# Both closing meetings of the engines placed ahead of GpSimd's wait for the last store

The kernel runs on one core of a Trainium2 chip (trn2). The metric is the time of one execution in device microseconds; each time of a kernel is a median of four to six runs (of the kernel before, up to eleven), and each stamp of a trace comes from one profiled run. All runs are fast (recorded clock 1.00).

## The reference

```python
def reference(x, y):            # both 1024 x 4096, float32
    z = x + y
    return (0.5 * z * (1 + np.tanh(np.sqrt(2 / np.pi) * (z + 0.044715 * z ** 3)))).astype(np.float32)
```

An addition and a GELU: 33.55 MB are read, 16.78 MB written.

## The kernel before

The arithmetic is split into 32 chunks of 128x1024: GpSimd adds (the first chunk is VectorE's), ScalarE squares and takes the sigmoid, VectorE does the two products. All loads and all five stores are issued by SyncE. None of this is touched. What is touched is the end of the program, which the framework writes and the kernel edits after compiling:

```python
    stores = [8192, 8192, 8192, 4096, 4096]      # elements per partition; the last is 2 MB in all
    ...
def wait_late(nc):
    body, end = nc.main_func.blocks[1:3]
    last = [i for i in body.instructions if isinstance(i, mybir.InstDMACopy)][-1]
    (sem,) = [u.id for u in last.sync_info.on_update]       # the last store's semaphore
    all_done = end.instructions[0]                           # SyncE's wait for everything
    clear = next(i for i in end.instructions if isinstance(i, mybir.InstDrain) and i.is_reset_sema)
    ...
    its = [w for w in waits if w.id == sem]
    rest = [w for w in waits if w.id != sem]
    ...
    at = end.instructions.index(clear)
    end.instructions[0] = drain(all_done, rest, is_reset_sema=False)
    end.instructions[at] = drain(clear, its, is_reset_sema=True, ...)
```

So the end block reads as follows. "Meeting" means: each of four engines adds 1 to a semaphore (96) and waits for another (97); GpSimd waits for the four, then releases them. In the trace of before the second meeting's four adds stand at 115.649 to 115.732 and the record of GpSimd's release at 120.430.

| SyncE | ScalarE, VectorE, TensorE | GpSimd |
|---|---|---|
| waits for all stores but the last | | |
| first meeting | first meeting | first meeting |
| | | drain that waits for the last store (semaphore 108) |
| | | range clear of semaphores 99 to 109 |
| second meeting | second meeting | second meeting: a drain, a wait for four, a release |

Behind that block the trace shows semaphore updates that match no record of the program: in the trace of before nine of semaphore 2 (120.769 to 121.294), one of each of the semaphores 7 to 255, but for a single missing record (121.193 to 121.860), and nine more of semaphore 2 (122.085 to 122.442). In all that follows, these are called the runtime's meeting (or first round), the sweep and the runtime's second round. The trace has no record of who makes these updates or what for.

## Time and profile before

| | before |
|---|---|
| three runs | 122.04, 122.37, 122.44 us |
| span, first to last instruction | 120.5 us |
| share of the DMA engines that the one queue fills | 98.1% |
| last increment of the last store | 120.013 |
| GpSimd's last record ends | 120.447 |
| last record of the span ends (TensorE) | 120.534 |
| runtime's first nine updates | 120.769 to 121.294 |
| runtime's second nine updates | 122.085 to 122.442 |

The stamps are starts or ends of records in the trace, in us from the start of the span. The last store's semaphore (108) gets 16 increments in the trace; at the last of them the store counts as landed here. It came 0.380 us after the last 16 KB packet's end (119.633 to 120.013). The last four rows are the tail in which no data moves. The measured time runs to about the last update of semaphore 2: in the profiled run the last update stood at 122.442 and the time was 122.32. So the tail counts in the measured time, beyond what the span shows.

### The profile page before, as it was taken

To read this page: it belongs to the slowest core of one execution; us is meant where nothing else is said; L and a number is where in the kernel's file an instruction comes from. 1 tells how busy PE (TensorE), PEld (TensorE's weight loads), DVE (VectorE), ACT (ScalarE), POOL (GpSimd) and SP (SyncE) were. 2 spreads that over 40 slices of the span, in tenths; PEclk is the share of its full clock that TensorE was granted. 3 is DMA by queue.
4 is the path that set the end of the run, shared out by engine and by line. 5 is a ranking of instruction groups with operands and counts; after the bars stand their busy time and mean duration, and the time that the engine had idled before them with its cause. 6 is when DMAs were issued, how large, how long until landed. Compare 5 with 4: busy or idle time off the path is not lost.

```text
span 120.5 us, 247 instructions
## 1 busy us (share of the span) xinstructions
DVE 75.5 (63%) x66; ACT 63.8 (53%) x66; POOL 73.0 (61%) x35
## 2 busy tenths in 40 slices
DVE  0044700059999009999996999995999999500000
ACT  4016200078875048788758888883878888100000
POOL 0056000699990299999979999949999990000000
DMA  6999999989898989898989899999999999998994
GB/s 201 430 457 449 440 416 446 468 381 489 348 522 348 522 348 522 348 511 359 500 370 489 381 478 391 359 402 459 394 468 402 468 402 468 391 478 364 430 435 174
DMA packets 2162, 50.35 MB, mean 418 GB/s; under 512 B 240, under 2 KB 240, under 8 KB 240
## 3 DMA queue, kind: packets, MB, share of 16 engines
q1 hardware_dynamic: 2160, 50.33, 98.1%
q14 instruction: 2, 0.02, 0.0%
HBM read 33.55 MB, written 16.78 MB: 418 GB/s over the span
## 4 chain that ended last, share of the span: by engine, by line
DMA 49%; POOL 17%; DVE 16%; SPq 1%; ACT 1%; issue 0%; POOLq 0%
DMA y<-in_y_dram 49%; POOL z L131 17%; DVE z L151 8%; DVE w L142 8%; ACT w L136 1%; SPq L114 1%; SPq L121 0%; POOLq L131 0%
## 5 line engine op out<-in xcount | busy, mean ns | idle before, releaser
L131 POOL TENSOR_TENSOR z<-z,y 128x1024 f32<-128x1024 f32 x31 | 72.8, 2387 | 26.3 <-DMA y<-in_y_dram 26.3
L142 DVE SCALAR_TENSOR_TENSOR w<-w,z 128x1024 f32<-128x1024 f32 x32 | 39.4, 1232 | 21.3 <-ACT w L136 21.3
L136 ACT ACTIVATE w<-z 128x1024 f32<-128x1024 f32 x32 | 32.9, 1028 | 37.5 <-POOL z L131 31.6
L151 DVE TENSOR_TENSOR z<-w,z 128x1024 f32<-128x1024 f32 x32 | 38.8, 1215 | 0.0
L147 ACT ACTIVATE w<-w 128x1024 f32<-128x1024 f32 x32 | 31.4, 981 | 0.4 <-DVE w L142 0.4
L131 DVE TENSOR_TENSOR z<-z,y 128x1024 f32<-128x1024 f32 x1 | 1.2, 1226 | 6.0 <-DMA y<-in_y_dram 6.0
L190 ACT ACT_TABLE_LOAD x1 | 1.3, 1283 | 1.3 <-PEq L222 1.3
L189 DVE MEMSET one<- 128x1 f32 x1 | 0.1, 59 | 1.3 <-PEq L222 1.3
L222 POOL MEMSET const-float32-0.0<- 128x1 f32 x1 | 0.1, 98 | 0.2 <-issue 0.2
L190 ACT ACTIVATE one<-one 128x1 f32<-128x1 f32 x1 | 0.2, 203 | 0.0
L222 POOL MEMSET const-bfloat16-1.0<- 128x1 bf16 x1 | 0.1, 101 | 0.0
L222 POOL MEMSET const-uint8-127<- 128x1 uint8 x1 | 0.1, 101 | 0.0
L222 POOL MEMSET const-float32-1.0<- 128x1 f32 x1 | 0.1, 98 | 0.0
## 6 DMA issues: line engine op xcount, KB each, us to landing
z<-in_x_dram SPq DMA_DIRECT2D x3, 4096.0 KB, 34.1
y<-in_y_dram SPq DMA_DIRECT2D x3, 4096.0 KB, 24.8
out_dram<-z SPq DMA_DIRECT2D x3, 4096.0 KB, 30.6
out_dram<-z SPq DMA_DIRECT2D x2, 2048.0 KB, 17.5
z<-in_x_dram SPq DMA_DIRECT2D x1, 3072.0 KB, 13.4
y<-in_y_dram SPq DMA_DIRECT2D x1, 3072.0 KB, 20.3
z<-in_x_dram SPq DMA_DIRECT2D x1, 1024.0 KB, 4.9
y<-in_y_dram SPq DMA_DIRECT2D x1, 1024.0 KB, 6.9
```

What stands on the lines that cost most here:

```text
L114: nc.sync.dma_start(out=zt[:, a:b], in_=xv[:, a:b])
L131: eng.tensor_add(out=zt[:, a:b], in0=zt[:, a:b], in1=yt[s][:, o : o + b - a])
L136: nc.scalar.activation(out=wt[c], in_=zt[:, a:b], func=act.Square, scale=root)
L142: nc.vector.scalar_tensor_tensor(out=wt[c], in0=wt[c], scalar=c1, in1=zt[:, a:b], op0=alu.add, op1=alu.mult)
L147: nc.scalar.activation(out=wt[c], in_=wt[c], func=act.Sigmoid)
L151: nc.vector.tensor_mul(out=zt[:, a:b], in0=wt[c], in1=zt[:, a:b])
L189: nc.vector.memset(one, 0.0)
L190: nc.scalar.activation(out=one, in_=one, func=act.Sigmoid)
L222: nc = _bacc.Bacc("TRN2", target_bir_lowering=False, num_devices=1)
```

## The change

Its intent: with the last store's wait and the clear behind both meetings, the second meeting can take place while the last store still runs, and GpSimd has only these two instructions left once it has landed. (The diffs here are cut; `...` stands for what is left out of a line.)

```diff
     at = end.instructions.index(clear)
+    clears = [drain(clear, its, is_reset_sema=True, ...), end.instructions[at + 1]]
+    assert isinstance(clears[1], mybir.InstISA) and clears[1].engine == POOL
+    del end.instructions[at : at + 2]
     end.instructions[0] = drain(all_done, rest, is_reset_sema=False)
-    end.instructions[at] = drain(clear, its, is_reset_sema=True, ...)
+    end.instructions.extend(clears)
```

More of the change, by code (lines that the diff above doesn't have):

```diff
@@ L47, in wait_late @@
     at = end.instructions.index(clear)
+    clears = [
+        drain(
+            clear, its, is_reset_sema=True,
+            reset_range_start=clear.reset_range_start, reset_range_stop=clear.reset_range_stop,
+        ),
+        end.instructions[at + 1],
+    ]
+    assert isinstance(clears[1], mybir.InstISA) and clears[1].engine == POOL
+    del end.instructions[at : at + 2]
     end.instructions[0] = drain(all_done, rest, is_reset_sema=False)
-    end.instructions[at] = drain(
-        clear, its, is_reset_sema=True,
-        reset_range_start=clear.reset_range_start, reset_range_stop=clear.reset_range_stop,
-    )
+    end.instructions.extend(clears)
 @with_exitstack
```

## The prediction

> **What bounds the kernel now.** I read the page from the top: span, engine shares, queues; then the busy time by stretch, the waits of the SyncE queue, and last every instruction of the closing line (L205), because that is all the change touches.
>
> ```profile
> span 120.5 us, 247 instructions
> DVE 75.5 (63%) x66; ACT 63.8 (53%) x66; POOL 73.0 (61%) x35
> ...
> q1 hardware_dynamic: 2160, 50.33, 98.1%
> ```
>
> No engine is busy for two thirds of the span, but the one DMA queue fills 98.1% of what 16 DMA engines have. 33.55 MB are read and 16.78 MB written, at 418 GB/s: the kernel is bound by its traffic, and the engines keep up. The busy time by stretch says it by stage (columns: stretch, length, DVE, ACT and POOL busy, clock, DMA share, GB/s):
>
> ```profile
> 0.00:104.50 104.50, 75.52 (x66) 63.76 (x66) 73.02 (x35) 1.00 1.00 425
> 104.50:120.04 15.54, 0.00 (x0) 0.00 (x0) 0.00 (x0) 1.00 0.89 384
> 120.04:120.60 0.56, 0.00 (x0) 0.00 (x0) 0.00 (x0) 1.00 0.00 0
> ```
>
> All arithmetic is over at 104.5. For 15.54 us the stores alone run. After that there are 0.56 us in which nothing moves and nothing computes: only sequencers talk. That last stretch is all that this change can reach inside the span. The page's chain that ended last stops at the last VectorE multiply (104.16), since it does not follow the sequencers, so it is of no use here. The waits of the SyncE queue are:
>
> ```profile
> SPq L125 <- DVE z L151: 42.1, 4, 19.7
> SPq L121 <- POOL z L131: 32.6, 2, 18.6
> SPq L121 <- DMA y<-in_y_dram: 22.7, 3, 14.6
> SPq L205 <- DMA out_dram<-z: 10.6, 2, 5.8
> SPq L205 <- PEq L205: 5.0, 2, 4.9
> ```
>
> The fourth row is SyncE waiting for the third-to-last and second-to-last stores at the end (5.8 and 4.8 us). The fifth is the wait in question: about 4.9 us in the second meeting of the engines, before its release (the engine named is only the last to arrive). The true holder is GpSimd, which waits for the last store before it goes to that meeting. The records of L205 from 120.03 on (durations in ns, first and last start in us):
>
> ```profile
> L205 POOLq DRAIN  x2: 34/58/83, 120.0 to 120.3; - x2
> L205 POOLq EVENT_SEMAPHORE  x2: 17/17/17, 120.4 to 120.4; - x2
> L205 POOLq EVENT_SEMAPHORE_RANGE_CLEAR  x1: 95/95/95, 120.1 to 120.1; - x1
> L205 SPq EVENT_SEMAPHORE  x1: 17/17/17, 120.5 to 120.5; - x1
> L205 ACTq EVENT_SEMAPHORE  x1: 17/17/17, 120.5 to 120.5; - x1
> L205 DVEq EVENT_SEMAPHORE  x1: 21/21/21, 120.5 to 120.5; - x1
> L205 PEldq EVENT_SEMAPHORE  x1: 51/51/51, 120.5 to 120.5; - x1
> ```
>
> With the stamps of the single records in the trace, the tail reads so. The last of the 16 increments of the last store comes at 120.013. GpSimd's waiting drain begins at 120.037 (83 ns), the clear at 120.149 (95 ns) and ends at **120.244**. Then GpSimd's own drain at 120.273 (34 ns), its wait for the four arrivals at 120.351 (17 ns; they came at 115.7), its release at 120.430 (17 ns, ends at 120.447). Then the four others leave: SyncE 120.471, ScalarE 120.475, VectorE and TensorE 120.483, the last ending at **120.534**.
>
> [...] after the kernel semaphore 2 gets nine updates from 120.769 to 121.294 (525 ns), then a sweep of semaphores, then nine from 122.085 to 122.442 (357 ns). The profiled run's time was 122.32 us, 1.8 more than its span, so I take this tail to be in the measured time. [...] GpSimd's three records between clear and release sum to 68 ns (34+17+17), but take 203 ns of time (120.244 to 120.447). So I count by starts and ends, not by durations. [...] the last 16 KB packet ended at 119.633 and the last increment came 380 ns later. The change leaves that alone.
>
> **The change part by part.** Nothing is removed or added: the built programs have the same instructions, apart from their order. On GpSimd two of them (the drain that waits for the last store, the range clear) go from between the meetings to the end. On the other four engines no order changes.
>
> 1. Up to the first meeting: nothing moves. All loads, arithmetic, stores and SyncE's waits stay; 0 us.
> 2. The second meeting now follows the first at once. In the trace before, the four arrive for it at 115.640 to 115.711, last increment 115.732. GpSimd's release follows some 0.1 us later, as in the first meeting (wait at 115.429, release ended 115.524). So everyone leaves by about 115.95 (estimate). This runs beside the last store, which lands 4 us later: free.
> 3. After the last store GpSimd has only the drain and the clear: by the stamps above it ends at 120.244. Taken off its path: 120.447 - 120.244 = **0.203 us**. Taken off the span, where TensorE's record ended last: 120.534 - 120.244 = **0.290 us**, so a span of 120.24.
> 4. The runtime's meeting follows. In its first round of semaphore 2 the gap between the second and third update is 205 ns, against 38 ns in the round with nobody late: one engine came 167 ns late. I can't see which. If it was GpSimd, its way from 120.447 to 121.008 takes 0.561 us; it stays on the path whole, and the gain is GpSimd's own 0.203. If it was another, that one now arrives 4.5 us early, and only GpSimd counts: with a way as short as 0.235 (TensorE's end at 120.534 to the first update at 120.769, an assumption) it arrives at 120.479, the rest of a round from its third update takes 0.285 (122.157 to 122.442), and the round ends at 120.764 in place of 121.294, a gain of 0.53.
>
> So 0.20 to 0.53 us, and I choose the span's own 0.29 as the middle, nearer the low end because GpSimd has the slowest drains (34 to 83 ns against 7 to 19 ns of the others) and is the likeliest late one. 122.37 - 0.29 = 122.08, which I put at **122.1 us**, 0.2% faster.
>
> **The rivals.** First: nothing at all is gained, because the runtime meets all the engines again anyway, and the second meeting's release is merely replaced by that. For it: the four others now wait in the runtime's meeting instead of the kernel's. Against it: GpSimd must pass both in series today, 0.203 us of which go. It would make 122.37. Second: the gain is much larger, since four engines could do their closing work (0.24 us for TensorE, the sweep of semaphores of 0.67 us from 121.193 to 121.860) under the store. For: they are idle for 4.5 us. Against: the sweep begins only once the runtime's meeting has GpSimd in it. If it did overlap, some 0.7 us more would go: 121.4. Third: it slows, because four engines go on to write or fetch through the DMA engines while the last store runs; a 32-byte fetch takes 7 ns in the trace and an 8 KB instruction page 309 to 559 ns on one of 16 engines. Two of these in the last 4 us would hardly show; at worst, if a page fell on the engine that lands last, +0.3 us: 122.4. Fourth: the traffic itself varies. The three times span 122.04 to 122.44, 0.40 us, larger than the effect; this can hide it but is no cause.
>
> **Range and chances.** Mechanism 0.20 to 0.53, the median's scatter about 0.2 each way: 121.75 to 122.45 should hold 8 times in 10. Two per cent are 2.4 us. All time in which no data moves after the last landing is 0.52 us in the span and 1.9 in the runtime's tail (120.534 to 122.442), so a gain over 2% would need all of it; a loss over 2% would need a store disturbed by 2.4 us, for which nothing speaks. Faster 0.01, same 0.98, slower 0.01.
>
> **What would show it.** Step 2: both meetings' records of L205 on SyncE, ScalarE, VectorE and TensorE all before 116.0, and SyncE's wait of 4.9 us at L205 gone. Step 3: the last record of the span is GpSimd's clear, 0.23 us after the last landing in place of 0.52. Step 4: the first round of semaphore 2 ends 1.0 us or less after the clear, with no late third update if GpSimd was not the late one. I am wrong if the median is unchanged over paired rounds although the span lost 0.29 (first rival), if it is below 121.75 (second), or if the last store lands later after its issue than 15.8 us (third).

Two statements got their figures from the traces afterwards: the sweep began 0.185 us after the third update of semaphore 2, which is GpSimd's, before (121.008 to 121.193) and after (120.426 to 120.611); and each of the five engines, when it waited for the last store, held up an update of the nine (the experiments). The 8 KB fetches took 309 ns inside the span of before, twice, and 307 to 559 ns ahead of it; that one would hold up a store on one of 16 DMA engines is the author's estimate and was not shown.

## The result

| | before | after |
|---|---|---|
| median of 6 runs | 122.25 us | 121.97 us |
| lowest, highest | 122.02, 122.50 | 121.73, 122.28 |
| ratio of after to before | | 0.9978 (0.9956 to 0.9999) |

A ratio here is the mean time of one kernel's fast runs over that of the other's fast runs of the same rounds, so it isn't quite the ratio of the medians. The gain is 0.2%, and the 95% interval barely leaves out 1. The scatter from run to run (0.5 us between the extremes, 122.02 and 122.50 before, 121.73 and 122.28 after) is larger than the effect, so the traces have to say whether it is real.

The page of the kernel after:

```profile
span 119.9 us, 247 instructions
DVE 75.5 (63%) x66; ACT 63.8 (53%) x66; POOL 73.0 (61%) x35
...
q1 hardware_dynamic: 2160, 50.33, 98.4%
```

Nothing has moved in the body: the busy times are those of before. The span is 0.6 us shorter, and this must not be taken as the gain: in this profile the last store landed at 119.675, in that of before at 120.013, which is 0.338 us of the traffic's own scatter. What follows the landing is the comparison to make. SyncE's waits after (rows: engine and line waiting, for whom, us in total, times, longest):

```profile
SPq L131 <- DVE z L157: 41.8, 4, 19.4
SPq L127 <- POOL z L137: 32.6, 2, 18.6
SPq L127 <- DMA y<-in_y_dram: 22.7, 3, 14.6
SPq L211 <- DMA out_dram<-z: 10.4, 2, 5.7
SPq L211 <- PEq L211: 0.4, 2, 0.3
```

L211 is the closing line, L205 of before. The wait of 4.9 us in the second meeting has become 0.3. The records of the closing line from 115 to 119 us, all under the last store (the first six of ten rows):

```profile
L211 POOLq EVENT_SEMAPHORE  x4: 17/17/17, 115.1 to 115.5; - x4
L211 SPq DRAIN  x2: 7/7/7, 115.0 to 115.3; - x2
L211 SPq EVENT_SEMAPHORE  x2: 17/17/17, 115.2 to 115.5; - x2
L211 ACTq EVENT_SEMAPHORE  x2: 17/17/17, 115.2 to 115.5; - x2
L211 DVEq EVENT_SEMAPHORE  x2: 21/21/21, 115.2 to 115.5; - x2
L211 PEldq EVENT_SEMAPHORE  x2: 51/51/51, 115.2 to 115.5; - x2
```

Two meetings within 0.6 us. And from the landing on, in place of the seven rows that the prediction shows of before:

```profile
L211 POOLq DRAIN  x1: 77/77/77, 119.7 to 119.7; - x1
L211 POOLq EVENT_SEMAPHORE_RANGE_CLEAR  x1: 95/95/95, 119.8 to 119.8; - x1
```

Now the same tail in both traces, in us from the last increment of the last store. The updates of semaphore 2 are stamps of the trace that the page doesn't show.

| from the last increment to | before | after | gain |
|---|---|---|---|
| GpSimd's last record ends | 0.434 | 0.225 | 0.209 |
| third update of semaphore 2 (GpSimd's way there: 0.561, 0.526) | 0.995 | 0.751 | 0.035 more |
| ninth update | 1.281 | 1.036 | 0.001 more |
| last update of the second nine | 2.429 | 2.181 | 0.003 more |
| sum | | | **0.248** |

The first two updates came 0.756 and 0.790 us after the landing in the trace of before; after, they came 3.850 and 3.816 us ahead of it, and the third waited for GpSimd. So the engine that came late for the third update, which the prediction couldn't name, is GpSimd: the only one with a record after the landing (its last ends 0.225 us after it; TensorE's, the last of the four others, 4.085 ahead of it).

### The profile page after: what moved, and what is told of

Its sections match the earlier page's. It is cut to its first block, busy times and chain, and to the rows that moved or that the text cites. A ratio compares the mean times of both kernels' runs of the same rounds, so it can differ in the third digit from the quotient of the medians.

```text
span 119.9 us, 247 instructions
## 1 busy us (share of the span) xinstructions
DVE 75.5 (63%) x66; ACT 63.8 (53%) x66; POOL 73.0 (61%) x35
## 3 DMA queue, kind: packets, MB, share of 16 engines
q1 hardware_dynamic: 2160, 50.33, 98.4%
## 4 chain that ended last, share of the span: by engine, by line
DMA 49%; POOL 17%; DVE 16%; SPq 1%; ACT 1%; issue 0%; POOLq 0%
DMA y<-in_y_dram 49%; POOL z L137 17%; DVE z L157 8%; DVE w L148 8%; ACT w L142 1%; SPq L120 1%; SPq L127 1%; POOLq L137 0%
```

## The experiments

The theory: the gain is what leaves GpSimd's own path between landing and the runtime's third update. The rival: it comes from the four other engines, which leave some 4.6 us earlier (relative to the landing) and can do their closing work under the store. A second rival is that it is scatter. Each kernel below is the changed one with the end block edited further; all gave correct results. The tail is taken from one profile each; where it was taken twice of one kernel (2.181 and 2.181, 1.519 and 1.515) it agreed to 0.004 us, so it resolves what the times can't.

| run | waiting engine's last record ends | its update of the nine | ninth update | last update | ratio to before (95%) |
|---|---|---|---|---|---|
| before | 0.434 | third, 0.995 | 1.281 | 2.429 | 1 |
| after | 0.225 | third, 0.751 | 1.036 | 2.181 | 0.9978 (0.9956 to 0.9999) |
| gp_three | 0.431 | third, 0.992 | 1.278 | 2.424 | 0.9992 (0.9973 to 1.0011) |
| no_second | 0.231 | third, 0.757 | 1.042 | 2.232 | 0.9977 (0.9957 to 0.9997) |
| gp_late | 2.170 | third, 2.694 | 2.979 | 4.126 | 1.0126 (1.0104 to 1.0148) |
| four_late | 0.225 | third, 0.752 | 1.039 | 2.184 | 0.9964 (0.9941 to 0.9988) |
| gp_waits | 0.041 | third, 0.610 | 0.895 | 2.041 | 0.9967 (0.9954 to 0.9979) |
| sp_waits | 0.034 | fifth, 0.175 | 0.339 | 1.483 | 0.9930 (0.9916 to 0.9943) |
| pe_waits | 0.079 | first, 0.354 | 0.713 | 1.858 | 0.9950 (0.9937 to 0.9962) |
| act_waits | 0.038 | second, 0.177 | 0.501 | 1.645 | 0.9948 (0.9934 to 0.9961) |
| after_again | 0.225 | third, 0.751 | 1.037 | 2.181 | 0.9980 (0.9966 to 0.9993) |
| dve_waits | 0.048 | fourth, 0.232 | 0.473 | 1.620 | 0.9941 (0.9929 to 0.9954) |
| sp_one_meeting | 0.034 | fifth, 0.169 | 0.333 | 1.519 | 0.9907 (0.9894 to 0.9921) |
| sp_one_again | 0.033 | fifth, 0.169 | 0.332 | 1.515 | 0.9927 (0.9909 to 0.9944) |

Columns two to five are us from the last increment of the last store. The waiting engine is the one that waits for the last store: GpSimd down to gp_waits.

### gp_three: the three instructions back, without the meeting

```diff
+    end.append(drain("I-9001", E.Pool))
+    end.append(event("I-9002", E.Pool, [], [up]))        # semaphore 96 plus 4
+    end.append(event("I-9003", E.Pool, [wait], [down]))  # wait for 4, take it off
```

> The changed kernel with three instructions added on GpSimd behind its clear: a drain, an add of 4 to a semaphore, a wait for that 4. They are the three that the change took from there, but nobody is met and no other engine waits. Theory (only GpSimd's own path counts): about 0.2 us come back; from the last store's last increment to the last update of semaphore 2 it takes 2.43 us as before the change (2.181 after it); ratio to the kernel before 0.999 to 1.001. Rival (the gain came from the four others leaving earlier): nothing comes back; 2.18 us, ratio 0.998.

Measured: 122.2 us against 122.31 (ratio 0.9992), tail 2.424. GpSimd's records from the landing on:

```profile
L238 POOLq DRAIN  x2: 34/56/77, 119.8 to 120.0; - x2
L238 POOLq EVENT_SEMAPHORE  x2: 17/17/17, 120.1 to 120.2; - x2
L238 POOLq EVENT_SEMAPHORE_RANGE_CLEAR  x1: 95/95/95, 119.9 to 119.9; - x1
```

These are GpSimd's five records of before, in another order of add and wait, but no other engine has a record there. The whole gain in the tail is gone (2.424 against 2.429), also the 0.035 us of the way into the runtime's meeting (0.561 again). The rival expected 2.18: it falls.

### no_second: the second meeting deleted

```diff
+    cut = [k for k, i in enumerate(end) if i.engine == E.Activation and isinstance(i, mybir.InstDrain)]
     ...
+    del end[cut[1] : len(end) - 2]
```

> The changed kernel without the second meeting: its 11 instructions are deleted. Theory: where the change has put it, the second meeting is free, under the last store, so deleting it brings nothing: 2.18 us from the last increment to the last update of semaphore 2, ratio 0.998, as the changed kernel. Rival (part of it still costs, or it did useful work): 0.1 us or more away from 2.18.

Measured: 122.1 us, ratio 0.9977; the nine updates are complete at 1.042 against 1.036. To the ninth update the second meeting is therefore free where the change has put it, and deleting it brings nothing more. One thing I can't explain: between the two rounds of the runtime, where it sweeps the semaphores, this kernel takes 0.833 us against 0.788. The two later kernels without the second meeting show it too (0.829, 0.826), all those with it 0.786 to 0.791. The trace places the 45 ns, without giving the cause: the sweep's updates run in five groups side by side (7 to 53, 54 to 104, 105 to 155, 156 to 206 and 207 to 255), and only the group up to 53, which ends last, starts later, 0.259 to 0.265 us after the ninth update in place of 0.215 to 0.221.

### gp_late and four_late: 24 drains on GpSimd, or on each of the four others

```diff
+    for k in range(24):
+        end.append(drain(f"I-{9000 + k}", E.Pool))              # gp_late
```
```diff
+    for j, e in enumerate((E.SP, E.Activation, E.DVE, E.PE)):
+        for k in range(24):
+            end.append(drain(f"I-{9000 + 100 * j + k}", e))      # four_late
```

> The changed kernel with 24 more drains on GpSimd behind its clear, an amplified load on its path. Theory: each costs its whole start to start time there, which I estimate at 75 ns (34 to 83 ns of record, some 30 to 40 ns to the next): +1.8 us on the changed kernel, about 123.8 us, ratio to before 1.013. Rival (GpSimd has slack before the runtime's meeting): less than 1 us.

> The changed kernel with 24 more drains on each of the four other engines, behind the second meeting. On SyncE two drains started 55 ns apart, so about 1.3 us each, ending near 117, before the last store lands near 119.7. Theory: no change, ratio 0.998 as the changed kernel, 2.18 us from the last increment to the end. Rival (the others' leaving counts): +1.3 us, ratio 1.009.

Measured: gp_late 123.92 us, ratio 1.0126; GpSimd's last record ends 1.945 us later than in the changed kernel (2.170 against 0.225) and the last update comes 1.945 later (4.126 against 2.181): what is added on GpSimd's path is paid whole.

```profile
L234 POOLq DRAIN  x25: 34/34/173, 120.0 to 122.1; - x25
L234 POOLq EVENT_SEMAPHORE_RANGE_CLEAR  x1: 95/95/95, 120.1 to 120.1; - x1
```

A drain with a record of 34 ns cost 61 ns from start to start here, less than my estimate of 75, which makes 1.46 us of the 24; one stall around the 15th, whose record is the 173 ns, added the other 0.48. This trace alone also has an 8 KB instruction fetch in the tail, but it begins at 122.134 us of the span, 0.53 us after the 15th drain's record ended; whether the two belong together is not shown. four_late: 121.85 us, ratio 0.9964, tail 2.184. The four end 2.3 to 3.3 us ahead of the landing in place of 4.1 (0.9 to 1.8 us later), and the tail is as without them. So after the change the four have slack, and their leaving early gains nothing. The first two were not waited for before the change either: there the third update came 0.205 us after the second, against 0.038 in the second round (122.119 to 122.157).

### gp_waits, sp_waits, pe_waits, act_waits, dve_waits: who waits for the last store

If only the waiting engine's path counts, another engine with a shorter path should do better than the change. GpSimd clears all semaphores but the last store's (108) in two range clears between the meetings, when nobody needs them any more. The engine on trial waits for 108 in one instruction that also takes the 32 off, so nothing is left uncleared:

```diff
+    end[cut[1] : cut[1]] = clears(0, a, s) + clears(1, s + 1, b)      # a, s, b: 99, 108, 110
+    down = mybir.SyncUpdate(..., id=s, ..., update_mode="sem-sub-imm", update_value=last.wait_value)      # 32
+    end.append(event("I-9020", E.SP, [last], [down]))      # or Pool, PE, Activation, DVE
```

> GpSimd clears all semaphores but the last store's between the two meetings (two range clears around it), and behind the second meeting waits for the last store in one semaphore instruction that also takes its 32 off. So behind the last increment GpSimd has one instruction in place of the drain and the clear. Theory (from the last increment to the end only the waiting engine's own records and its way into the runtime's meeting count): last record ends 0.05 us after the last increment in place of 0.225, then 0.53 us to the third update as before, 2.01 us to the last update of semaphore 2 against 2.18; ratio to before 0.9965. Rival (the clear costs nothing there): 2.18, 0.998.

> As gp_waits, but SyncE has the waiting instruction. GpSimd is done 4 us earlier and its 0.53 us into the runtime's meeting run under the store. Theory: only SyncE's way counts; if that is the 0.235 us of TensorE, and SyncE gives a late update of the nine (the fourth or fifth), the nine are complete 0.5 us after the last increment against 1.04 in the changed kernel, 1.7 us to the end, ratio to before 0.994. Rival (every engine's way into the meeting takes 0.53 us): 2.0 us, as gp_waits.

> As gp_waits, but TensorE has the waiting instruction. It gives the first update of the nine 0.235 us after its last record. Theory: last record ends 0.08 us after the last increment, first update at 0.31, the nine take 0.37 from there, so complete at 0.68 against 1.04; 1.82 us to the end, ratio to before 0.995. Rival as in sp_waits: 2.0 us or more.

> As gp_waits, but ScalarE has the waiting instruction. Its place in the runtime's meeting is not known: with a way of 0.235 us the nine are complete at 0.5 to 0.6 us after the last increment, 1.65 to 1.75 us to the end, ratio to before 0.994 to 0.9945. Rival as in sp_waits: 2.0 us.

> As sp_waits, but VectorE has the waiting instruction. TensorE, ScalarE, GpSimd and SyncE gave the first, second, third and fifth update in the runs before, so VectorE gives the fourth. With a way of 0.14 us as SyncE's and ScalarE's, the fourth update comes 0.19 us after the last increment, the nine are complete at 0.43, 1.57 us to the end, ratio to before 0.9935: between sp_waits (1.483) and act_waits (1.645). A different place in the order would put it outside those two.

Measured, in that order: 121.74, 121.36, 121.50 and 121.53 us against 122.11 before, and dve_waits 121.57 against 122.24. The records of the closing line from the landing on are a single one, GpSimd's in gp_waits and SyncE's in sp_waits:

```profile
L257 POOLq EVENT_SEMAPHORE  x1: 17/17/17, 119.8 to 119.8; - x1
```
```profile
L257 SPq EVENT_SEMAPHORE  x1: 17/17/17, 120.0 to 120.0; - x1
```

gp_waits takes the waiting drain and the clear off GpSimd's path and gains 0.140 us in the tail over the changed kernel: 0.184 by the last record, less 0.043 that the way to the third update became longer (0.569 against 0.526). Moving the same instruction to SyncE gains another 0.558 (2.041 to 1.483): 0.428 by the shorter way, 0.121 because less of the meeting comes behind SyncE's update, 0.009 by the rest. The rival of equal ways falls. From the end of the waiting record to that engine's update it took GpSimd 0.569 us, TensorE 0.275, VectorE 0.184, SyncE 0.141 and ScalarE 0.139; and an engine with a late place in the nine has fewer updates after its own: to the ninth it took 0.359 us from TensorE's, 0.324 from ScalarE's, 0.285 from GpSimd's, 0.241 from VectorE's and 0.164 from SyncE's. How many updates come ahead of the landing shows the places: none with TensorE waiting, one with ScalarE, two with GpSimd, three with VectorE, four with SyncE. SyncE has both a short way and the last place of the five; ScalarE's way is as short, and its second place alone makes its tail 0.162 longer. My numbers were off: 1.7 for sp_waits (measured 1.483), because I gave SyncE TensorE's way of 0.235; 2.01 for gp_waits (2.041), 1.82 for pe_waits (1.858) and 1.57 for dve_waits (1.620) were a few hundredths short.

### after_again and sp_one_meeting, sp_one_again: the pairing, and the best version

sp_one_meeting is sp_waits with the second meeting deleted, two lines more, of which the second is:

```diff
+    del end[second:-1]      # from ScalarE's drain of the second meeting up to SyncE's wait
```

> The changed kernel, unaltered, for a pairing with the two others of this call on the same chip. 2.18 us from the last increment to the last update of semaphore 2, ratio to before 0.998.

> sp_waits with the second meeting deleted: one meeting, GpSimd's two clears, and SyncE's wait for the last store. Theory: the second meeting is free there, so this is sp_waits again: 1.48 us from the last increment to the end, ratio to before 0.993, and 0.5 per cent below the changed kernel of the same rounds. Rival (the meeting counted): under 1.45 us.

> sp_one_meeting once more, because its ratio (0.9907) was lower than sp_waits' (0.993) although its tail was 0.036 us longer in the trace (1.519 against 1.483). Theory (chance in when the last store lands, which differed by 0.3 us between profiles): tail 1.52 again, ratio to before 0.992 to 0.994. Rival (the deleted meeting makes the stores land earlier): ratio 0.991 or less again.

after_again repeats the change: 121.97 us against 122.24, ratio 0.9980 with an interval of 0.9966 to 0.9993, tail 2.181. So the gain is there a second time, away from 1. sp_one_meeting gave 121.09 us, better than expected, though its tail was longer than that of sp_waits (1.519 against 1.483). Run again, it gave 121.36 us and 0.9927, as sp_waits. In the first profile the last store landed at 119.631, in the second at 120.081: the traffic's scatter is enough for the surplus, which did not come again. That it was chance is likely and not shown; no_second, where the same meeting is deleted, had no surplus over the changed kernel (0.9977 against 0.9978).

The best version is therefore either of the two with SyncE waiting: sp_waits, 121.36 us against 122.11 before, ratio 0.9930, tail 0.946 us shorter than before and 0.698 shorter than the changed kernel's. The second meeting makes no difference to it that these runs could show.

## Why the prediction was right

It said 122.1 us (121.75 to 122.45) and "same"; measured 121.97.

- **Traffic bounds the kernel and isn't touched**: right. The one queue fills 98.1% of the DMA engines before and 98.4% after, while no engine is busy for more than 63% of the span. Busy times are equal to 0.1 us, and the last store took as long from the end of its issue as before (103.968 + 0.332 to 119.675, 15.4 us; before 104.189 + 0.332 to 120.013, 15.5 us). The third rival, disturbed stores, has nothing for it: the trace's last instruction fetch begins at 85.9 us, 29 us ahead of the meetings.
- **Step 2, the second meeting is free under the store**: right; SyncE's wait of 4.9 us became 0.3, and no_second shows that deleting it gains nothing to the ninth update.
- **Step 3, 0.203 us off GpSimd's path and 0.290 off the span after the landing**: measured 0.209 and 0.296 (0.521 to 0.225); the 6 ns more are the waiting drain's record, 83 before and 77 after. The predicted span of 120.24 became 119.9 by an earlier landing, which the step doesn't explain.
- **Step 4, how much of it reaches the end**: this was left open between 0.20 and 0.53. The branch "if it was GpSimd" is the true one: 0.209 plus 0.035 that its way became shorter plus 0.004 of the rest, 0.248 in the tail. The term I mis-sized is that way: I carried it over as 0.561, and it measured 0.526. It varies with GpSimd's last instruction: it was 0.561 to 0.569 in the five kernels where that is a semaphore instruction (gp_three and gp_waits among them), and 0.524 to 0.534 in the seven runs where it is the clear or a drain. The other branch, 0.53, rested on a way of 0.235 for GpSimd and is refuted; GpSimd's was never under 0.524. That my 0.29 meets the medians' difference of 0.28 is partly luck: the tail says 0.25, and the times can't tell the two apart. The 0.29 was what TensorE's end leaves of the span, which is not on the path to the third update; my own reason for the low end, that GpSimd was the late one, gives 0.203.
- **First rival, nothing gained**: refuted by the tail and by after_again. **Second rival, the others' closing work under the store**: two of their updates did move there (3.85 us ahead of the landing), but the third is GpSimd's, so it gained nothing; gp_three and four_late show it.

What stays open is what GpSimd does for 0.53 us between its last instruction and its update, where SyncE needs 0.14: the profile has no record in that stretch.

## What to carry to other kernels

In this kernel, once the last transfer had landed, only the path of the engine that waits for it counted, up to its update in the runtime's meeting and what follows there: take off that engine whatever can be done before, and try the wait on another engine, since the ways into that meeting differ (0.14 to 0.57 us here). Count such a tail from the landing, by starts and ends, in the trace of each kernel, since the scatter of the transfers (the last landing differed by 0.338 us between before and after) hides a quarter of a microsecond in the times. To see whose path it is, add a load to the engine in question, and then to the others: 1.945 us on GpSimd came back in full, 0.9 to 1.8 on the four others together not at all, as long as they ended ahead of the landing.

## What the traces show of the tail's parts

- The nine updates of semaphore 2 took 357 ns from first to ninth in the second round of before, with nobody late, and 525 ns in the first, where GpSimd was late. The steps of the second round were 34, 38, 44, 24, 98, 38, 34 and 47 ns. From the ninth update to the first of the next round it took 0.79 us, and 0.89 from the first update of the sweep.
- The order of the engines in the first five updates: TensorE, ScalarE, GpSimd, VectorE, SyncE, by the five runs in which one of them waited for the last store.
- From the end of an engine's last record to its update: ScalarE 0.139 us (act_waits), SyncE 0.135 to 0.141 (sp_one_meeting, sp_waits), VectorE 0.184 (dve_waits), TensorE 0.235 to 0.275 (before, pe_waits), GpSimd 0.524 to 0.569 (gp_late, gp_waits). With the place in the order this made 0.56 us between the best and the worst choice of the waiting engine (1.483 and 2.041), 0.43 of it by the way.
- Three records of GpSimd, 68 ns together, took 203 ns before the change. A GpSimd drain of 34 ns cost 61 ns from start to start (gp_late), a semaphore record of 17 ns on the same engine 79 (before, 120.351 to 120.430).
- The stall of 0.4 us in the midst of 24 equal drains on GpSimd (gp_late, 1.045 to 1.444 us from the landing, from one start to the next) was seen once and is not explained.
